# The sums of xT's blocks in the widening stages: from GpSimd to VectorE

## The chip, the core and the metric

The kernel runs on one core of a Trainium2 chip. The metric is the time of one execution on the device, in microseconds (us). In the profile the engines are PE (TensorE's matmuls; PEld is its weight loads), DVE (VectorE), ACT (ScalarE), POOL (GpSimd) and SP (SyncE, which here issues loads from HBM).

## The reference

Two transformer-like blocks are computed on x of 512 tokens by 1024 channels, in float32. What matters here are the three places where a wide pair of projections (1024 to 2 x 2816) feeds a gate:

```python
def swiglu(x, w_gate, w_up, w_down):
    return (jax.nn.silu(x @ w_gate) * (x @ w_up)) @ w_down
...
def _conv_ffn(x, w_in, conv_w, conv_b, w_out):
    s = x.shape[1]
    u = x @ w_in
    up = jnp.pad(u, ((0, 0), (CONV_WIDTH_2 - 1, 0), (0, 0)))
    u = sum(conv_w[j] * up[:, j:j + s] for j in range(CONV_WIDTH_2)) + conv_b
    g, val = u[..., :D_FF_2], u[..., D_FF_2:]
    return (jax.nn.silu(g) * val) @ w_out
```

swiglu is in the first block; _conv_ffn comes twice, once after each attention of the second block.

## The kernel before

Every float32 matmul is three passes on high and low parts (hi x hi, hi x lo, lo x hi): `split` (L182) makes the high part with an ACT copy (L183) and the low part with a subtraction on DVE (L185). Weights come as tiles `raw` (SP loads), are split into `wh` and `wl`, 128x1024 each, and go to PE; a small pool of such pieces is released as PE finishes with them. The normed input, transposed, is in xT: `xh` and `xl`, each in two tiles of four rows of 128 channels (order lists the tiles as xh_5119 and xh_5120 in stage two).

A widening stage is `wide` (L776). There are three: in `block1_ffn` (about 190 to 440 us, "stage one"), and in `conv_ffn` (from about 797 us, "stage two", and from about 1411 us, "stage three"; these two run the same code). Each has 22 chunks of 128 gate and 128 value channels:

- The first four chunks (`f_phase`, the lead) are plain products into PSUM tiles `fa`. In the first two of them PE also turns the last tokens into xT (tiles `pt`).
- The other 18 are `fast_chunk`: a Strassen-like scheme with seven smaller products per chunk instead of eight. In order they use the operands g[2], g[1], g[5], g[6], g[7], g[4], g[3]. Product 1 fills half of PSUM tile `c` (c2), and ACT copies it out to `m` (m2, L519). Product 2 fills tile `p` (p1). Product 3 goes to the other half of c2, and waits for the copy m2.

The operands g are made by `sums` (L465). It first adds high and low parts of xT's four blocks (L474: 4 additions of 128x1024), then makes five sums or differences of these, z1 to z5 (L483: 5 more), kept in unused rows of `hT`. Each z is then split (L183 and L185) into an operand: z1 to `g1h`/`g1l`, z2 to `g6h`/`g6l`, z3 to `g7h`/`g7l`, z4 back into the second tile of xT (g[4]) and z5 into the first (g[3]).

For the weights of the fast chunks, sums are needed too: an accumulating DMA on POOL's queue (L274) and then two additions of 128x512 on POOL (L277 and L278, recorded as L176, `raw`<-`raw`); ACT's copy to `wh` waits for these. In stages two and three POOL also multiplies gate and value (L1011, recorded as L176, `hT`<-`hT`,`tv`), and each PSUM tile is emptied by an ACT pass (L1002) and two DVE passes ("taps", L1003 and L1004). In stage one there is one DVE multiplication (L967) per chunk instead.

The order on each engine is fixed at build time by a scheduler with priorities; PE's order is written out by hand. An engine takes its instructions strictly in that order. `issue_after` and `behind` bind only this order.

Of the kernel before, what the change touches and what calls it, by code (L numbers as in the profile page):

```python
# [99 lines left out]
class Net:  # L100
# [675 lines left out]
    def wide(self, hT, evac):  # L776

        with ExitStack() as fs:
            pool, self.fz = (fs.enter_context(self.tc.tile_pool(name=n, bufs=1)) for n in ("sums", "fz"))
            self.f_phase(LEAD, evac)  # L780

            rows = lambda r: hT[:, r:r + 2, :].rearrange("p a (b c) -> p (a b) c", c=256)
            tmp = [rows(NF - KD + 2 * i) for i in range(4)]
            zs = [lambda i=i: rows(LEAD + 2 * i) for i in range(5)]
            new = lambda n: tuple(pool.tile([P, 4, 256], F32R, name=f"g{n}{e}") for e in "hl")
            b = {}
            with self.behind(3), self.tc.issue_after(self.powed.ins):
                for _ in self.sums(b, new, tmp, zs):
                    pass
            with self.tc.manual_schedule(engines={mybir.EngineType.PE}):  # L790
                for c in range(LEAD, NF):
                    if c == NF - 1:
                        self.operands = 0
                        self.ahead = [self.pair(hT, 0)]
                    ps = {}
                    for _ in self.fast_chunk(b, ps.__setitem__, True):
                        pass
                    evac(c, ps[0], ps[1])
# [774 lines left out]
```

## Time and profile before

| | |
|---|---|
| median of 3 runs | 1767.71 us (1765.19 to 1772.61) |
| the profiled execution: its time | 1769.7 us |
| its span in the trace | 1767.9 us |
| TensorE clock granted, mean of the span | 0.98 |
| PE busy | 1671.8 us, 95% of the span |
| DVE busy | 1438.4 us, 81% |
| ACT busy | 1011.4 us, 57% |
| POOL busy | 757.6 us, 43% |

The span is a little shorter than the time, since the time also holds what lies around the recorded instructions. A busy share is an average over stages with different limits.

### The profile page before, as it was taken

The numbers are of one execution on the slowest core, as the hardware profiler recorded it, in microseconds if no ns is written. First come the engines' busy times: TensorE is split into PE (matmuls) and PEld (weight loads), VectorE is DVE, ScalarE is ACT, GpSimd is POOL, SyncE is SP. The second block draws the span as 40 slices with busy tenths as digits, with TensorE's granted clock in tenths as the row PEclk, the third lists the DMA queues.
The fourth block names the chain that finished last, engine by engine and source line by source line (L and its number), as shares of the span: only waits on it lengthen the run. The fifth ranks groups of instructions, "written<-read, shape, count | busy, mean of one in ns | idle before, by whom it ended". The sixth has DMA issues, their size and how long they took to land. (4 is left out here: it accounts for less than half of the span.)

```text
span 1767.9 us, 28040 instructions
## 1 busy us (share of the span) xinstructions
PE 1671.8 (95%) x10432; PEld 1486.2 (84%) x10432; DVE 1438.4 (81%) x2159; ACT 1011.4 (57%) x1733; POOL 757.6 (43%) x528
## 2 busy tenths in 40 slices
PE   6977999999999999999999998999998999999996
PEld 6856999999788889879999987787776799999875
DVE  5985677678877789967899899855888679998999
ACT  6662445455563677745666564644667455656553
POOL 2485643330023365218555527344232185566522
PEclk9988999999999999989999999999999999999998
DMA  6469566668978665744566689797543335666553
GB/s 233 170 187 246 154 161 179 192 180 282 351 218 220 166 158 149 203 109 136 154 181 178 179 283 333 218 238 193 124 114 89 97 98 156 182 194 185 191 184 107
DMA packets 106072, 326.05 MB, mean 184 GB/s; under 512 B 9888, under 2 KB 10016, under 8 KB 93904
## 3 DMA queue, kind: packets, MB, share of 16 engines
q1 hardware_dynamic: 73088, 215.53, 35.6%
q0 software_dynamic: 25648, 73.54, 22.3%
q10 hardware_dynamic: 7200, 35.20, 5.5%
q8 instruction: 82, 1.34, 0.3%
q14 instruction: 54, 0.44, 0.1%
HBM read 274.91 MB, written 73.43 MB: 197 GB/s over the span
## 5 line engine op out<-in xcount | busy, mean ns | idle before, releaser
L183 ACT ACTIVATE wh<-raw 128x1024 fp32r<-128x1024 f32 x457 | 450.8, 998 | 405.4 <-PE c L437 100.3
L185 DVE TENSOR_TENSOR wl<-raw,wh 128x1024 fp32r<-128x1024 f32 (+1 forms) x415 | 528.4, 1287 | 132.2 <-ACT wh L183 125.8
L436 PE MATMUL c<-xh,wh 128*128 128x256 f32 x992 | 283.5, 286 | 8.8 <-ACT m L519 8.8
L176 POOL TENSOR_TENSOR raw<-raw 128x512 f32<-128x512 f32 x124 | 180.6, 1456 | 247.0 <-DMA raw<-raw 207.3
L437 PE MATMUL c<-xl,wh 128*128 128x256 f32 x992 | 282.5, 285 | 0.0
L438 PE MATMUL c<-xh,wl 128*128 128x256 f32 x992 | 281.9, 284 | 0.0
L436 PEld LDWEIGHTS c<-xh,wh 128*128 128x128 f32 x992 | 190.7, 192 | 10.7 <-ACT m L519 10.5
L437 PEld LDWEIGHTS c<-xl,wh 128*128 128x128 f32 x992 | 190.7, 192 | 0.2
L438 PEld LDWEIGHTS c<-xh,wl 128*128 128x128 f32 x992 | 190.7, 192 | 0.0
L438 PE MATMUL dn<-wh,hl 128*128 128x512 f32 x462 | 181.6, 394 | 7.7 <-DVE hl L185 7.6
L437 PE MATMUL dn<-wl,hh 128*128 128x512 f32 x462 | 181.8, 395 | 2.5 <-DVE wl L185 2.4
L436 PE MATMUL dn<-wh,hh 128*128 128x512 f32 x462 | 179.2, 394 | 0.1
L150 POOL COPY paced<-wh 128x1 f32<-128x1 f32 x48 | 35.6, 741 | 232.1 <-ACT wh L183 232.0
L436 PE MATMUL fa<-xh,wh 128*128 128x256 f32 (+1 forms) x400 | 133.0, 333 | 1.6 <-ACT wh L183 1.6
L437 PE MATMUL fa<-xl,wh 128*128 128x256 f32 (+1 forms) x400 | 132.6, 332 | 1.1 <-DVE xl L185 1.1
L438 PE MATMUL fa<-xh,wl 128*128 128x256 f32 (+1 forms) x400 | 132.5, 331 | 0.8 <-DVE wl L185 0.8
L176 POOL TENSOR_TENSOR wl<-raw,wh 128x1024 fp32r<-128x1024 f32 (+1 forms) x42 | 97.2, 2319 | 83.3 <-ACT wh L183 80.4
L176 POOL TENSOR_TENSOR hT<-hT,tv 128x512 f32<-128x512 f32 x44 | 102.8, 2336 | 37.3 <-DVE tv L1004 37.3
L176 POOL TENSOR_TENSOR rs_r<-rs_t,mhalf 128x1 f32<-128x1 f32 (+1 forms) x40 | 32.0, 800 | 195.1 <-DVE rs_t L326 193.6
L438 PEld LDWEIGHTS dn<-wh,hl 128*128 128x128 f32 x462 | 87.5, 189 | 27.7 <-DVE hl L185 9.7
L437 PEld LDWEIGHTS dn<-wl,hh 128*128 128x128 f32 x462 | 87.8, 190 | 23.7 <-DVE wl L185 5.8
L436 PEld LDWEIGHTS dn<-wh,hh 128*128 128x128 f32 x462 | 87.7, 190 | 18.8 <-ACT wh L183 0.5
(305 smaller groups left out, 4573.7 us busy)
## 6 DMA issues: line engine op xcount, KB each, us to landing
raw<-in_w_conv_dram SPq DMA_DIRECT2D x36, 1024.0 KB, 4.9
mixed<-in_narrow_dram ACTq DMA_DIRECT2D x48, 704.0 KB, 6.5
raw<-raw POOLq DMA_DIRECT2D x62, 512.0 KB, 5.1
raw<-mixed SPq DMA_DIRECT2D x51, 512.0 KB, 5.9
raw<-in_narrow_dram SPq DMA_DIRECT2D x48, 512.0 KB, 5.8
raw<-in_w_ffn_dram SPq DMA_DIRECT2D x18, 1024.0 KB, 4.9
mixed<-in_narrow_dram POOLq DMA_DIRECT2D x24, 704.0 KB, 10.1
mixed<-mixed POOLq DMA_DIRECT2D x24, 704.0 KB, 9.5
```

The costliest lines, as they stand in the source:

```text
L150: paced = self.nc.gpsimd.tensor_copy(m, self.ready[-1][0][:, 0:1].bitcast(F32))
L176: self.pooled = self.nc.gpsimd.tensor_tensor(*args, **kw)
L183: self.copied = self.nc.scalar.activation(hi, src, AF.Copy)
L185: return self.copied, sub(lo, src, hi.bitcast(F32), op=ALU.subtract)
L436: mm(ps, lh, rh, start=first, stop=False)
L437: mm(ps, lh, rl, start=False, stop=False)
L438: mm(ps, ll, rh, start=False, stop=last)
```

## The change

`sums` is given VectorE's tensor_tensor for its additions, where it used GpSimd's.

```diff
@@ def wide
             with self.behind(3), self.tc.issue_after(self.powed.ins):
-                for _ in self.sums(b, new, tmp, zs):
+                for _ in self.sums(b, new, tmp, zs, self.nc.vector.tensor_tensor):
                     pass
```

In `sums` (unchanged) the argument decides who adds:

```python
        gp = engine or self.pool
        for x, (k, q) in zip(tmp, ((A, t), (A, u), (B, t), (B, u))):
            h, l = here(k, q)
            gp(x, h.bitcast(F32), l.bitcast(F32), op=ALU.add)
```

So nine additions of 128x1024 in each of the three stages leave POOL and enter DVE's order. PE's and SP's orders are the same as before; ACT's and DVE's change around the first fast chunk, and POOL's loses the nine rows.

DVE in stage two, a piece of the difference (lines with + are of the change). The place is from the emptying of the lead's second chunk on.

```order
 L1003 SCALAR_TENSOR_TENSOR tv<-fa,vec,tv 128x511
+L474 TENSOR_TENSOR hT<-xh_5119,xl_5121 128x1024
+L1004 SCALAR_TENSOR_TENSOR tv<-fa,vec,tv 128x510
+L474 TENSOR_TENSOR hT<-xh_5119,xl_5121 128x1024
+L474 TENSOR_TENSOR hT<-xh_5120,xl_5122 128x1024
+L185 TENSOR_TENSOR wl<-raw,wh 128x1024
+L1003 SCALAR_TENSOR_TENSOR hT<-fa,vec,hT 128x511
+L474 TENSOR_TENSOR hT<-xh_5120,xl_5122 128x1024
+L1004 SCALAR_TENSOR_TENSOR hT<-fa,vec,hT 128x510
+L483 TENSOR_TENSOR hT<-hT 128x1024
+L185 TENSOR_TENSOR wl<-raw,wh 128x1024
```

The additions now stand between the taps and the weight splits of the lead's chunks, and the other four L483 rows follow in the same manner, all ahead of g1l.

ACT in stage two before, the last rows up to m2 (the row m_8765, which product 3 waits for):

```order
L183 ACTIVATE xh_5119<-hT 128x4x256
L1010 ACTIVATE hT<-hT 128x512
L183 ACTIVATE wh<-raw 128x512
L1002 ACTIVATE tv<-fa,vec 128x512
L183 ACTIVATE xh_5120<-hT 128x4x256
L519 ACTIVATE m_8765<-c_8762 128x256
```

Four instructions stood between the copy of z5 (xh_5119) and m2. The same place in the change:

```order
L183 ACTIVATE g7h<-hT 128x1024
L183 ACTIVATE xh_5119<-hT 128x4x256
L183 ACTIVATE wh<-raw 128x512
L1002 ACTIVATE tv<-fa,vec 128x512
L1010 ACTIVATE hT<-hT 128x512
L183 ACTIVATE xh_5120<-hT 128x4x256
L519 ACTIVATE m_8765<-c_8762 128x256
```

The rows are the same; g7h has moved up to just ahead of xh_5119, and the gate function (L1010) back behind the tap.

## Rows read from the trace of the kernel before

**Rows 1.** The page, part 1: busy time, share of the span, instructions.
```profile
PE 1671.8 (95%) x10432; PEld 1486.2 (84%) x10432; DVE 1438.4 (81%) x2159; ACT 1011.4 (57%) x1733; POOL 757.6 (43%) x528
```

**Rows 2.** PE's waits in stage one, 176 to 340 us: total, times, longest.
```profile
PE pt L337 <- DVE y L357: 0.2, 1, 0.2
```

**Rows 3.** PE's waits in stage two, 780 to 960 us.
```profile
PE c L436 <- ACT m L519: 2.6, 1, 2.6
...
PE pt L337 <- DVE X L391: 0.2, 1, 0.2
```

**Rows 4.** PE's waits in stage three, 1380 to 1560 us.
```profile
PE c L436 <- ACT m L519: 2.9, 1, 2.9
...
PE pt L337 <- DVE X L391: 0.4, 1, 0.4
```

**Rows 5.** PE's timeline around the wait in stage two: start, length, instruction.
```profile
845.84 0.28 PE L437 MATMUL p<-g1l,wh 128*128 128x256 f32 x1
...
849.91 0.39 PE L436 MATMUL c<-xh,wh 128*128 128x256 f32 x1 [2.59 <-ACT m L519]
```

**Rows 6.** Two windows behind the waits: length, busy us (instructions) per engine, PEclk.
```profile
850.90:854.32 3.42, 3.42 (x18) 3.42 (x18) 3.30 (x5) 1.06 (x1) 2.50 (x2) 0.50 0.71 156
1465.31:1468.72 3.41, 3.41 (x18) 3.41 (x18) 2.99 (x4) 1.06 (x1) 2.01 (x2) 0.50 0.87 178
```

**Rows 7.** ACT's timeline in stage two.
```profile
840.40 1.06 ACT L183 ACTIVATE wh<-raw 128x1024 fp32r<-128x1024 f32 x1 [0.26 <-POOL raw L176]
...
843.63 1.05 ACT L183 ACTIVATE xh<-hT 128x1024 fp32r<-128x1024 f32 x1
846.83 0.63 ACT L1010 ACTIVATE hT<-hT 128x512 f32<-128x512 f32 x1 [2.14 <-DVE hT L1004]
...
849.49 0.37 ACT L519 ACTIVATE m<-c 128x256 f32<-128x256 f32 x1
```

**Rows 8.** DVE's timeline in stage two.
```profile
815.08 2.91 DVE L185 TENSOR_TENSOR wl<-raw,wh 128x1024 fp32r<-128x1024 f32 x1 [5.26 <-ACT wh L183]
817.92 0.74 DVE L1003 SCALAR_TENSOR_TENSOR hT<-fa,vec,hT 128x511 f32<-128x511 f32 x1
...
819.36 1.99 DVE L185 TENSOR_TENSOR wl<-raw,wh 128x1024 fp32r<-128x1024 f32 x1
...
828.64 1.65 DVE L185 TENSOR_TENSOR g1l<-hT,g1h 128x1024 fp32r<-128x1024 f32 x1
...
836.68 1.29 DVE L185 TENSOR_TENSOR wl<-raw,wh 128x1024 fp32r<-128x1024 f32 x1 [3.46 <-ACT wh L183]
...
841.49 1.22 DVE L185 TENSOR_TENSOR wl<-raw,wh 128x1024 fp32r<-128x1024 f32 x1 [2.08 <-ACT wh L183]
```

**Rows 9.** POOL's timeline in stage two.
```profile
814.51 12.46 POOL L176 TENSOR_TENSOR hT<-hT 128x1024 f32<-128x1024 f32 x4
826.93 2.28 POOL L176 TENSOR_TENSOR hT<-hT,tv 128x512 f32<-128x512 f32 x1
829.16 1.24 POOL L274 DMA_DIRECT2D raw<-raw  x1
835.59 1.29 POOL L176 TENSOR_TENSOR raw<-raw 128x512 f32<-128x512 f32 x1 [5.20 <-DMA raw<-raw]
```

**Rows 10.** POOL's groups by shape, whole span: the sums of the three stages.
```profile
L176 POOL TENSOR_TENSOR hT<-hT 128x1024 f32<-128x1024 f32 x15 | 47.2, 3176 | 0.2
...
L176 POOL TENSOR_TENSOR hT<-xh,xl 128x1024 f32<-128x1024 f32 x12 | 29.4, 2468 | 2.7 <-PE pt L337 2.7
```

**Rows 11.** The additions of `sums` on DVE in the first attention: ns min/median/max.
```profile
L474 DVE TENSOR_TENSOR sum<-xh,xl x4: 1211/1214/1216, 534.8 to 542.3; 128x1024 f32<-128x1024 f32 x4
...
L483 DVE TENSOR_TENSOR sum<-sum x5: 1214/1216/1226, 544.6 to 572.7; 128x1024 f32<-128x1024 f32 x5
```

**Rows 12.** DVE's timeline in stage one: the split of z1.
```profile
220.70 3.42 DVE L185 TENSOR_TENSOR g1l<-hT,g1h 128x1024 fp32r<-128x1024 f32 x1
```

**Rows 13.** PE's timeline in stage one: product 2 of the first fast chunk.
```profile
238.09 0.28 PE L437 MATMUL p<-g1l,wh 128*128 128x256 f32 x1
```

## Prediction

> **What bounds the kernel now.** I read the page first: PE is busy for 95% of the span, DVE for 81% [rows 1]. So the change can only act on time in which PE waits, and the next view is PE's waits, stage by stage. In stage one there is one of 0.2 us [rows 2]. In stages two and three one wait stands out, 2.6 and 2.9 us, for ACT's copy m2 [rows 3, 4]; the rest is 0.2 and 0.4 us for the normed X before a transposition. The wait has a second price. In the window right behind it the granted clock is 0.50, the lower of the two levels, for 3.41 us in each stage [rows 6]; PE does half as much in it, which loses 1.7 us. So the two waits cost 2.6 + 2.9 + 2 x 1.7 = 8.9 us together, 0.5% of the time, and 9.5 with the small waits for X. This is all that there is to gain.
>
> Why is m2 late? Follow it back through four timelines. ACT ran m2 at 849.49, as the last of a row of instructions that began at 846.83, and that first one had waited 2.14 us for a DVE tap [rows 7]. DVE was late because its weight splits had waited for `wh`, 3.46 us at 836.68 and 2.08 at 841.49 [rows 8]. The second `wh`, at 840.40, had waited for POOL's addition of raw weights [rows 7]; the first of these additions started at 835.59, behind an accumulating DMA that POOL issued at 829.16, and POOL got there only after its sums (the last four ended at 814.51 + 12.46 = 826.97) and one multiplication [rows 9]. So today's wait does begin at the sums on POOL. The question is what takes their place.
>
> **The change, part by part.** *Removed:* 27 additions on POOL, 47.2 + 29.4 = 76.6 us of its time [rows 10]. POOL is not a bound, so this alone is worth nothing; what counts is that the DMA goes out earlier. It still needs its own weights loaded first, into a `raw` buffer that DVE frees with the split at 819.36 [rows 8], so the bounds are no gain and 829.16 - 821.35 = 7.8 us (821.35 is the end of that split). I take 4.5 as an estimate, in the middle: issued near 824.7, landed 6.4 us later as today [rows 9], near 831.
>
> *Added:* nine additions on DVE in each stage. The same operation on the same shape ran there in the first attention, 1.21 us each [rows 11]: 9 x 1.215 = 10.9 us a stage.
>
> *Given back:* two things. Under POOL's sums DVE's weight splits were slow, 2.91 us once and 1.99 three times in stage two, against 1.22 at 841.49 [rows 8]: 1.7 + 3 x 0.77 = 4.0 us come back. And the two waits for `wh`, 3.46 + 2.08 = 5.5 us, can be filled with additions, since `wh` comes earlier; by the new order I expect about 2 us of idle time to stay (before `wh` copies that wait for PE to release pieces or for the landing at 831; the bounds are 0 and the 5.5 of today).
>
> *Moved:* by DVE's new order the splits g1l, g6l and g7l come behind the taps of the last gate tile, where they were ahead of them: 1.65 + 2 x 1.2, some 4 us that no longer delay this tap, but delay g1l itself. In ACT's new order the copy of z5 (xh_5119) is followed by four instructions and then m2, so m2 now hangs on z5, the last addition.
>
> *The unknown:* DVE's additions read two operands from SBUF, as the slow weight splits do, and POOL still has some seven operations of 128x512 in that stretch (multiplications and raw additions). How much each costs DVE is shown by no row of before. Bounds from the nearest rows: nothing at the lower end (the split at 836.68 took 0.07 us more than 1.22 with POOL at work), and 1.29 us each at the upper end, if each addition waits out a whole POOL operation [rows 8, 9]: 0 to 9.0 us. I take 0.3 each, 2 us: between 0.07 and the 0.77 that was seen beside a POOL that ran without a gap, and nearer to the first, since the operations left are short and apart.
>
> *The sum, for stage two.* Let T be the end of the DVE tap that ACT waited for, today about 846.8 [rows 7]. T = 846.8 + 10.9 - 4.0 - 4.1 - 5.5 + 2.0 + 2.0 = 848.1. z5 ends one tap earlier, 0.75 before T. From there ACT needs one split copy, about 1.0 (1.05 in the row at 843.63), and then what it needed from 846.83 to 849.49, 2.66 [rows 7]: m2 starts at T + 2.9 = 851.0, 1.5 us later than today. g1l is ready at T + 1.2 = 849.3, where PE wants it at 845.84 [rows 5]: product 2 now waits 3.5 us as well, and what is left of the wait for m2 stands behind it. The low clock I leave as today. Behind product 3, PE is fed about as it was, since DVE's later splits slide with T. So a stage loses 1.5 us; stage three runs the same code and loses the same.
>
> Stage one: g1l ended at 224.1 while PE wanted it at 238.09 [rows 12, 13]. Even 10.9 us more, with no relief counted, would fit into these 14 us, and DVE has no taps there. I put it at zero.
>
> The small waits for X (0.2 and 0.4) stand under POOL's first sums and shrink: -0.4.
>
> Total: 2 x 1.5 - 0.4 = +2.6 us. The profiled execution took 1769.7, so it would take 1772.3; it lies 2.0 above the median of the runs, 1767.71, on which I put the same difference: **1770.3**.
>
> **Rivals.** *The waits vanish* (faster). If T falls to 844.4 or below, m2 is there when product 2 ends (847.3) and g1l nearly in time. Then both waits, both stretches of low clock and the small waits go: 1767.7 - 9.5 = 1758.2. It needs 3.7 us less than my sum: no idle time left on DVE and hardly a collision. For it speaks that the chain that makes m2 late today begins at POOL; against it, that DVE, which must now do the sums ahead of the same tap, has no room. The Trainium skill's page "GPSIMD Engine Reference" (section "Engine selection") says that additions of two tensors belong on VectorE, GpSimd being about twice as slow. The trace agrees, 1.21 against 2.47 and 3.18 us [rows 10, 11], and by that rule alone this rival would be the outcome. What it leaves out is the queue that the additions join. 0.11.
>
> *The wait splits in two and the clock stays up.* Part falls on product 2 and part on product 3; if neither brings the low clock, 2 x 1.7 comes off: 1766.9. It needs pieces shorter than the 2.6 that was enough for it today, and I expect 3.5 on product 2. 0.20.
>
> *DVE is the new bound* (slower). Place: the same additions; mechanism: collisions with POOL. It decides from 5 us of collisions on, of 9.0 possible: then T is 851.1, a stage loses 4.6, and the total passes +8.8. With 7 us: T = 853.1, 6.6 a stage, 1767.7 + 13.2 - 0.4 = 1780.5. For it speaks the 1.99 and 2.91; against it, that POOL runs with gaps once its sums are gone. 0.14.
>
> **How the numbers follow.** The forecast itself, a small loss of 0 to 8 us, has 0.55. A measurement here can tell about 0.5%, 8.8 us, from no change. The forecast and the split wait lie within it, as do the weak ends of the other two: faster 0.10, same 0.77, slower 0.13. The range goes from 1761 (collisions near nothing, one of the two waits gone) to 1778 (5 us lost a stage), and leaves out the cores of the first and last rivals, 2 in 10.
>
> **What would show it.** In the changed profile: the additions at about 1.2 to 1.6 us on DVE; the accumulating DMA of stage two issued near 825 instead of 829; a PE wait on g1l (DVE, L185) at product 2 and one on m2 behind it, together 3 to 6 us a stage; no new wait in stage one. The forecast is wrong if PE runs through products 2 and 3 without a wait, or if the additions take 2 us and more and PE waits there for 8.

## The result: 1.0% slower, and the profile after

The changed kernel takes 1786.49 us (median of 6 runs, 1780.92 to 1789.14); the kernel before, run beside it, takes 1768.3 (6 runs). The ratio is 1.0098, 95% interval 1.0083 to 1.0113: some 18 us slower. The forecast of 1770.3 and its range, which ended at 1778, are missed. The profiled execution took 1784.89 us, its span is 1782.8.

The page's part 1 after the change answers to [rows 1]:

```profile
PE 1671.0 (94%) x10432; PEld 1485.2 (83%) x10432; DVE 1442.3 (81%) x2186; ACT 1010.9 (57%) x1733; POOL 684.0 (38%) x501
```

POOL is busy 73.6 us less (757.6 before), since its 27 additions are gone. DVE now has them, and yet its total is only 3.9 us higher: its weight splits no longer run beside POOL's sums. By these totals the exchange is a bargain. PE's busy time is the same. The loss must be in what PE waits for, so its waits come next, those of stage one first, then of stages two and three (they answer to [rows 2 to 4]; total, times, longest):

```profile
PE p L437 <- DVE g1l L185: 2.2, 1, 2.2
PE c L438 <- DVE wl L185: 1.0, 1, 1.0
PE c L436 <- DVE y L527: 0.5, 1, 0.5
...
PE p L437 <- DVE g1l L185: 6.9, 1, 6.9
PE c L437 <- DVE xl L185: 1.6, 2, 1.1
...
PE p L437 <- DVE g1l L185: 6.6, 1, 6.6
PE c L437 <- DVE xl L185: 1.7, 2, 1.2
```

The wait for m2 is gone. In its place product 2 waits for g1l, as forecast, but for 6.9 and 6.6 us instead of 3.5, and in stage one too, where nothing was expected. DVE's timeline in stage two shows what g1l stood behind (the answer to [rows 8]):

```profile
815.33 1.22 DVE L185 TENSOR_TENSOR wl<-raw,wh 128x1024 fp32r<-128x1024 f32 x1 [5.26 <-ACT wh L183]
...
821.78 1.67 DVE L185 TENSOR_TENSOR wl<-raw,wh 128x1024 fp32r<-128x1024 f32 x1 [0.89 <-ACT wh L183]
...
826.60 1.22 DVE L474 TENSOR_TENSOR hT<-xh,xl 128x1024 f32<-128x1024 f32 x1
...
828.39 2.35 DVE L474 TENSOR_TENSOR hT<-xh,xl 128x1024 f32<-128x1024 f32 x2
834.73 1.29 DVE L185 TENSOR_TENSOR wl<-raw,wh 128x1024 fp32r<-128x1024 f32 x1 [3.98 <-ACT wh L183]
...
836.60 1.65 DVE L474 TENSOR_TENSOR hT<-xh,xl 128x1024 f32<-128x1024 f32 x1
...
838.84 1.65 DVE L483 TENSOR_TENSOR hT<-hT 128x1024 f32<-128x1024 f32 x1
...
844.13 2.35 DVE L483 TENSOR_TENSOR hT<-hT 128x1024 f32<-128x1024 f32 x2
846.40 2.29 DVE L185 TENSOR_TENSOR wl<-raw,wh 128x1024 fp32r<-128x1024 f32 x1
848.61 0.74 DVE L1003 SCALAR_TENSOR_TENSOR hT<-fa,vec,hT 128x511 f32<-128x511 f32 x1
849.27 1.62 DVE L483 TENSOR_TENSOR hT<-hT 128x1024 f32<-128x1024 f32 x1
850.82 0.73 DVE L1004 SCALAR_TENSOR_TENSOR hT<-fa,vec,hT 128x510 f32<-128x510 f32 x1
851.48 1.63 DVE L185 TENSOR_TENSOR g1l<-hT,g1h 128x1024 fp32r<-128x1024 f32 x1
```

Two things are to be seen. An addition on an undisturbed DVE takes about 1.2 us, as forecast. But after the first three, DVE stands idle for 3.98 us in front of a weight split, with six more additions queued behind it. And several rows are longer than 1.21 (a pair: 2.35): 0.46 + 0.08 + 0.44 + 0.44 + 1.08 + 0.41 + 0.42 = 3.3 us from 821.78 to the end of g1l. The taps, whose first operand is in PSUM, never are.

POOL's timeline says what the split waited for (the answer to [rows 9]), and below it are ACT's copies `wh` and m2 (to [rows 7]):

```profile
825.05 1.24 POOL L274 DMA_DIRECT2D raw<-raw  x1 [2.68 <-issue]
833.65 1.29 POOL L176 TENSOR_TENSOR raw<-raw 128x512 f32<-128x512 f32 x1 [7.36 <-DMA raw<-raw]
834.90 2.27 POOL L176 TENSOR_TENSOR hT<-hT,tv 128x512 f32<-128x512 f32 x1
837.14 2.27 POOL L176 TENSOR_TENSOR raw<-raw 128x512 f32<-128x512 f32 x1
```

```profile
833.64 1.06 ACT L183 ACTIVATE wh<-raw 128x1024 fp32r<-128x1024 f32 x1 [8.02 <-PE fa L437]
...
854.60 0.36 ACT L519 ACTIVATE m<-c 128x256 f32<-128x256 f32 x1
```

The accumulating DMA goes out at 825.05, 4.1 us earlier than before, as forecast (near 825). But it lands only at 833.65, 8.6 us later instead of 6.4: of the 4.1 us gained, 1.9 are left. The copy `wh` starts within a hundredth of it. The row names PE as its releaser, but the run without a first sum and without products, below, shows that PE had freed the piece long before.

Last, the clock in the windows from the wait on (the answer to [rows 6]):

```profile
846.20:848.90 2.70, 0.04 (x1) 0.00 (x0) 2.70 (x3) 1.01 (x2) 2.62 (x2) 1.00 0.00 0
848.90:853.10 4.20, 0.00 (x0) 0.00 (x0) 4.20 (x5) 2.11 (x3) 3.12 (x2) 0.50 0.73 250
853.10:859.14 6.04, 5.98 (x28) 5.98 (x29) 5.03 (x8) 2.75 (x5) 2.80 (x2) 0.50 0.67 133
```

PE stands from 846.2 to 853.1. The granted clock falls to 0.50, its lower level of 1.2 GHz, during the wait, and stays there for 6.04 us of work after it, where it was 3.41 before. So the second price of the wait grew from 1.7 to 3.0 us.

### The profile page after: what moved, and what is told of

It is laid out like the page before. It is cut to its first block, busy times and chain, and to the rows that moved or that the text cites. A ratio compares the mean times of both kernels' runs of the same rounds, so it can differ in the third digit from the quotient of the medians.

```text
span 1782.8 us, 28043 instructions
## 1 busy us (share of the span) xinstructions
PE 1671.0 (94%) x10432; PEld 1485.2 (83%) x10432; DVE 1442.3 (81%) x2186; ACT 1010.9 (57%) x1733; POOL 684.0 (38%) x501
## 5 line engine op out<-in xcount | busy, mean ns | idle before, releaser
L185 DVE TENSOR_TENSOR wl<-raw,wh 128x1024 fp32r<-128x1024 f32 (+1 forms) x415 | 494.1, 1204 | 135.6 <-ACT wh L183 132.2
L274 POOL DMA_DIRECT2D raw<-raw x62 | 74.1, 1195 | 121.5 <-DMA raw<-in_w_ffn_dram 33.0
```

Of the source, the lines that this page charges most:

```text
L185: return self.copied, sub(lo, src, hi.bitcast(F32), op=ALU.subtract)
L274: self.nc.gpsimd.dma_start(out=raw[:, 0:4:2, :], in_=raw[:, 1:4:2, :], accum_op=ALU.add)
```

## Experiments

Two theories. A (order): the additions on DVE stand in a strict order behind a weight split, which waits for the late DMA. B (collisions): DVE's additions and splits and POOL's operations hold each other up, and that is the main cost.

### One stage at a time

```diff
-    def wide(self, hT, evac):
+    def wide(self, hT, evac, engine=None):
...
-                for _ in self.sums(b, new, tmp, zs, self.nc.vector.tensor_tensor):
+                for _ in self.sums(b, new, tmp, zs, engine):
...
-            self.wide(hT, evac)
+            self.wide(hT, evac, nc.vector.tensor_tensor)
```

The last line stands in `block1_ffn` in the first of the two kernels, in `conv_ffn` in the second.

> VectorE makes the sums in stage one alone; GpSimd makes them again in stages two and three. The changed kernel's profile puts 4.6 us of its 18 us loss in stage one: PE waits 2.2 us for g1l, 1.0 for a weight split and 0.5 for y there, where it had waited 0.2. Theory A (order: the additions on VectorE stand behind a weight split that waits for the accumulating DMA) and theory B (collisions of VectorE with GpSimd) both say that stage one pays by itself: 1768 + 4.6 = about 1773 us. The prediction's own step (14 us of slack, so stage one costs nothing) says 1768. The loss of stages two and three is expected to be gone in both.

> VectorE makes the sums in stages two and three; GpSimd makes them again in stage one. If the stages add up, this costs 7.5 + 6.8 = 14.3 us: about 1782.5 us, and with the run of stage one alone the two losses sum to the 18 us of the whole change. If something carries over from stage one into the later ones (or the other way), they don't sum: under 1780 or over 1786.

Stage one alone: 1774.2 us, ratio 1.0027 (1.0015 to 1.0039), 4.8 us of 1768.75. Stages two and three alone: 1785.15 us, ratio 1.0083 (1.0067 to 1.0098), 14.7 us. The two sum to 19.5, against 17.3 for the whole change (0.98% of the same 1768.75); the intervals are some 2 us wide on either side, so the stages add up. In the first kernel PE's waits in stage one are those of the change (2.2, 1.0, 0.5) and those of stages two and three are the old ones (2.7 for m2). So the prediction's zero for stage one is wrong, whatever happens in the later stages.

### The first weight sum as an addition on POOL

```diff
-        self.nc.gpsimd.dma_start(out=raw[:, 0:4:2, :], in_=raw[:, 1:4:2, :], accum_op=ALU.add)
+        gp(raw[:, 0:4:2, :], raw[:, 0:4:2, :], raw[:, 1:4:2, :], op=ALU.add) if first else self.nc.gpsimd.dma_start(out=raw[:, 0:4:2, :], in_=raw[:, 1:4:2, :], accum_op=ALU.add)
```

`first` is true for the first weight block of each widening stage. DVE's, ACT's and PE's orders are those of the change.

> The changed kernel, but the first weight sum of each widening stage, an accumulating DMA, is one addition of 128x1024 on GpSimd; VectorE's, ScalarE's and PE's orders are the same as in the change. Theory A (the late DMA holds the copy wh, this holds a weight split on VectorE, and this holds the additions behind it, 4.0 us in stage two and 5.6 in stage one): the split no longer waits, product 2 waits some 4 us less in stages two and three, the stretch at the low clock becomes shorter, and the wait of stage one goes. 1786.5 - 3.7 - 2 x (4 to 7.4) = 1768 to 1775 us. Theory B (collisions are the main cost): one more operation of GpSimd with two operands in the same stretch, so no gain or a loss: 1786 to 1791 us.

1783.74 us, ratio to the kernel before 1.0085 (1.007 to 1.01): hardly better than the change. Theory A expected at most 1775 and falls as it stood; theory B expected 1786 or more and is missed too. The profile says why. DVE's timeline in stage two, and POOL's below it:

```profile
824.11 3.27 DVE L185 TENSOR_TENSOR wl<-raw,wh 128x1024 fp32r<-128x1024 f32 x1
...
827.96 1.66 DVE L474 TENSOR_TENSOR hT<-xh,xl 128x1024 f32<-128x1024 f32 x1
...
830.20 3.88 DVE L474 TENSOR_TENSOR hT<-xh,xl 128x1024 f32<-128x1024 f32 x2
834.01 1.21 DVE L185 TENSOR_TENSOR wl<-raw,wh 128x1024 fp32r<-128x1024 f32 x1
...
850.80 1.21 DVE L185 TENSOR_TENSOR g1l<-hT,g1h 128x1024 fp32r<-128x1024 f32 x1
```

```profile
823.91 6.87 POOL L176 TENSOR_TENSOR raw<-raw 128x1024 f32<-128x1024 f32 x3 [2.24 <-issue]
830.73 2.28 POOL L176 TENSOR_TENSOR hT<-hT,tv 128x512 f32<-128x512 f32 x1
```

The stall in front of the split at 834.01 is gone, as A said. But POOL's three additions run just where DVE's do, and DVE's rows are now 7.1 us over length, instead of 3.3 (0.45 in a split at 821.10, 2.06 + 0.45 + 1.53 in the rows above, then 1.10, 0.44 and 1.08 up to g1l). One loss took the place of the other, and product 2 still waits 6.5 us for g1l. In stage one the same edit did help: the wait for g1l is gone and 0.5 us each for a weight split and for y are left. There too collisions took the place of the stall (the four L474 rows run for 9.02 us instead of 4.63), but by less: 6.0 us of rows over length, against 5.62 of stall and 3.3 over length in the change.

### Leaving the losses out, one by one

To see both losses apart, POOL's work was left out. Without the lead's products of gate and value:

```diff
-                self.pool(g, g, v, op=ALU.mult)
+                c < LEAD or self.pool(g, g, v, op=ALU.mult)
```

> The changed kernel without GpSimd's products of gate and value for the lead's four chunks in stages two and three (so part of the hidden layer is not gated). The DMA and GpSimd's weight sums stay. By the changed trace some 0.9 us a stage of the 2.9 us of collisions lie beside these products, and the wait of VectorE behind the DMA, 4.0 us, stays. If VectorE is simply full (every us of stall ahead of g1l falls on the tensor engine), the wait for g1l goes from 6.9 to about 6.0 us: 1783 to 1786 us. If collisions were the main cost, it would be halved: under 1780.

Without the first block's weight sums:

```diff
-        self.nc.gpsimd.dma_start(out=raw[:, 0:4:2, :], in_=raw[:, 1:4:2, :], accum_op=ALU.add)
+        first or self.nc.gpsimd.dma_start(out=raw[:, 0:4:2, :], in_=raw[:, 1:4:2, :], accum_op=ALU.add)
...
-            gp(two[:, 1, :], raw[:, 2, :], raw[:, 1, :], op=ALU.add)
-            gp(two[:, 2, :], two[:, 1, :], two[:, 0, :], op=ALU.add)
-            return [two[:, 1:3, :].rearrange("p s c -> p (s c)")], None
+            for j, x, y in [] if first else [(1, raw[:, 2, :], raw[:, 1, :]), (2, two[:, 1, :], two[:, 0, :])]:
+                gp(two[:, j, :], x, y, op=ALU.add)
+            return [flat[:, 1024:] if first else two[:, 1:3, :].rearrange("p s c -> p (s c)")], None
```

> The changed kernel without any sum for the first weight block of each widening stage: neither its accumulating DMA nor its two additions on GpSimd (so the first fast chunk multiplies unsummed weights). Last time the DMA's stall was removed, and three additions on GpSimd came in its place with 7.2 us of collisions against 2.9. Here both go, and what is left are GpSimd's products, about 2.6 us a stage. If stall and collisions are two parts of one bound, a full VectorE, the wait for g1l goes from 6.5 to about 2 us, with a short stretch at the low clock or none: 1764 to 1774 us. If neither is the cause: 1782 us or more.

And with both edits:

> Both left out, the first block's weight sums and the lead's products: VectorE has its additions, splits and taps and nearly nothing to collide with. Its work from the split at 821.1 on to the end of g1l is 23.9 us without a stall, so g1l would be there at about 845, when product 2 wants it (845.8): no wait for g1l, 1759 to 1768 us. If a wait of several us stays, the additions cost more than stalls and collisions explain.

They took 1785.28 us (ratio 1.0099, 1.0074 to 1.0123), 1775.64 (1.0045, 1.0032 to 1.0058) and 1766.31 (0.9991, 0.9976 to 1.0007). The third equals the kernel before. The second lies a little above its 1764 to 1774: its wait was 2.9 us and not about 2. In stage two, with the over-length rows added up as above:

| kernel | DVE idle before the split that the DMA held | rows over length, to g1l's end | sum | PE's wait for g1l |
|---|---|---|---|---|
| the change | 4.0 | 3.3 | 7.3 | 6.9 |
| no products | 5.3 | 2.1 | 7.4 | 6.9 |
| first sum on POOL | 0 | 7.1 | 7.1 | 6.5 |
| no first sum | 0 | 3.6 | 3.6 | 2.9 |
| neither | 0 | 1.2 | 1.2 | 0.6 |

The last column is read from PE's waits in stage two; below are the rows of the last four kernels, in this order:

```profile
PE p L437 <- DVE g1l L185: 6.9, 1, 6.9
PE p L437 <- DVE g1l L185: 6.5, 1, 6.5
PE p L437 <- DVE g1l L185: 2.9, 1, 2.9
PE p L437 <- DVE g1l L185: 0.6, 1, 0.6
```

The wait is the sum less 0.4 to 0.7 us in all five. Stage three repeats this with another mixture: in the change the stall is 2.98 us there (the DMA took 7.9) and 4.0 us are over length, 7.0 together, for a wait of 6.6; with neither, 1.1 us are over length and the wait is 0.4. So DVE, with the sums in this place, has about half a us of slack before product 2 wants g1l, and whatever holds it, a stall or a collision, reaches PE in full. This is the result of the study. Theories A and B are two parts of one bound, and neither is the cause alone.

Two rows need a word. The run without products met its number (1783 to 1786) by luck, for another reason than expected: the collisions shrank by 1.2 us, but its DMA landed 9.7 us after its issue and the stall grew by 1.3. And the run with neither has this in DVE's timeline:

```profile
829.27 1.22 DVE L185 TENSOR_TENSOR wl<-raw,wh 128x1024 fp32r<-128x1024 f32 x1
...
844.65 1.21 DVE L185 TENSOR_TENSOR g1l<-hT,g1h 128x1024 fp32r<-128x1024 f32 x1
```

The split that had waited 3.98 us follows the additions without a gap. Its copy `wh` starts at 827.23, when PE frees a piece; so in the changed kernel, which is 0.95 us later there (its split at 815.33 against 814.38), PE had freed it by about 828.2, and the 5.4 us to 833.64 were the DMA's.

### Another order in the same place

```diff
-            with self.behind(3), self.tc.issue_after(self.powed.ins):
+            with self.behind(3), self.tc.issue_after(self.powed.ins), self.tc.high_priority(offset=250):
```

> The changed kernel with the additions and the splits g1l, g6l and g7l at high priority, still held behind the third group of later work: the additions stand in a row, one weight split between the fourth and the fifth, then the three splits, and the taps that stood between them come after. The sum of VectorE's work from there to the copy m2 is the same. Full VectorE: the wait for g1l goes, but the taps are later, so the lead's PSUM tiles or m2 are late instead: 1778 to 1788 us. If only the place of g1l behind the last tap cost the time: 1768 us or less.

1792.93 us, ratio 1.0145 (1.0117 to 1.0172): above the full-DVE theory's 1778 to 1788, but by its mechanism. The wait for g1l is gone in stages two and three (in stage one product 2 waits 3.6 us for a weight split instead), but the taps now stand behind the sums, and the lead's PSUM tiles come free late (stage two):

```profile
PE fa L436 <- DVE tv L1004: 12.1, 1, 12.1
```

It is longer than the wait it replaced, since all eight taps stand behind nine additions and three splits. A stretch of 13.65 us at the low clock began within it. So this other arrangement of the same work in the same place only moved the wait; no third one was tried.

### Another place

```diff
-            with self.behind(3), self.tc.issue_after(self.powed.ins):
+            with self.tc.issue_after(self.powed.ins):
```

> The changed kernel, but the scheduler isn't told to hold the additions behind the third group of later work, so they stand on VectorE right after (partly between) the splits that make xT, where it was idle for 5.3 us in stage two and 8.3 in stage one; the split g6l comes earlier too. Theory A (a place in the order decides): additions and splits no longer wait behind the weight split that the DMA holds, and g1l and m2 are ready in time: 1762 to 1772 us, so most of the loss is gone. Theory B (collisions): only the collisions of the additions, 2.9 us a stage by the sum over stage two, can go: 1786.5 - 3 x 2.9 = 1778 us or more. A loss beyond 1787 would say that the splits of xT, now partly behind additions, make PE wait at the start of the lead.

1761.95 us (9 runs), ratio to the kernel before 0.9958 (0.9945 to 0.9971): 7.4 us faster than before and, by the medians, some 24 faster than the change. PE's waits in stage two, and DVE's timeline there:

```profile
PE fa L437 <- DVE xl L185: 0.6, 1, 0.6
PE c L436 <- ACT m L519: 0.2, 1, 0.2
```

```profile
802.21 1.21 DVE L474 TENSOR_TENSOR hT<-xh,xl 128x1024 f32<-128x1024 f32 x1
...
812.96 1.23 DVE L474 TENSOR_TENSOR hT<-xh,xl 128x1024 f32<-128x1024 f32 x1
...
814.70 1.21 DVE L483 TENSOR_TENSOR hT<-hT 128x1024 f32<-128x1024 f32 x1
...
833.71 1.28 DVE L185 TENSOR_TENSOR wl<-raw,wh 128x1024 fp32r<-128x1024 f32 x1 [1.85 <-ACT wh L183]
...
836.23 2.25 DVE L185 TENSOR_TENSOR g1l<-hT,g1h 128x1024 fp32r<-128x1024 f32 x1
```

Six additions now run from 802 to 817. There DVE had idled for want of weights (5.26 us before 815.33 in the changed kernel), and POOL, with nothing to do between 807.4 and 825.9, leaves them at 1.17 to 1.23 us. Only three stand later. The split still waits for the DMA, 1.85 us, but g1l ends at 838.5, long before it is wanted. The stretch at the low clock is gone with the wait. DVE's busy time is the change's, 1442.3 us to the tenth. (This edit moves some of PE's instructions too: the last eight transpositions stand behind 65 of the lead's products in this trace, and behind 48 in the changed kernel's.)

Two more runs bound this. The same release with the sums on POOL (the edit above, in the kernel before):

> The kernel before (sums on GpSimd), with the same release as the run of the early sums: nothing holds the sums behind the third group of later work. By the order GpSimd's own row stays as it was, and on VectorE the splits g6l, g1l and g7l move up to right behind xT's last split, ahead of the lead's first weight splits. Does the early place pay by itself, without VectorE's additions? Theory (place and engine belong together): the sums need some 29 us on GpSimd, so these splits wait until about 830 in stage two, the lead's weight splits wait behind them, and the tensor engine stands for 12 to 20 us a stage and more at the low clock: 1768 + 3 x (12 to 25) = 1804 to 1843 us. If the place alone gave the gain: 1765 us or less.

1797.64 us, ratio 1.0164 (1.0137 to 1.0191): the early place costs 28 us without the fast engine. The mechanism is the expected one, but smaller than expected: the split g6l waits 8.20 us for POOL's sums, with the lead's weight splits behind it, and PE waits 8.1 us for the lead's tiles in stage two. And the early sums on DVE together with the first weight sum on POOL:

> The early sums on VectorE, and the first weight sum of each stage as one addition on GpSimd in place of the accumulating DMA. VectorE's order is that of the early sums. In that run the tensor engine's waits in the three stages are down to 0.2 and 0.6 us, so there is nothing left to win: 1760 to 1764 us, the same as the early sums alone (1762) if the stall behind the DMA (1.9 us on VectorE there) has become slack. If the added collisions reach g1l, 1765 us or more.

1762.2 us, ratio 0.996 (0.9944 to 0.9977): the same as the early sums alone. With DVE's work moved away, the stall behind the DMA is slack.

## Why the prediction was wrong, point by point

- **What bounds the kernel, and what would follow m2.** Right in the main. PE lost its time at product 2, on g1l, and the wait for m2 disappeared behind it, wholly, where the sum had left 2.6 + 1.5 - 3.5 = 0.6 us of it. The DMA went out near 825, and an addition costs about 1.2 us (a pair 2.35). One reading was incomplete: before the change PE also waits 0.6 us for xl of the lead in each of stages two and three, which "all that there is to gain" leaves out. These waits are there after the change too.
- **The step that failed: "about 2 us of idle time to stay".** It was 0.22 + 0.89 + 3.98 = 5.1 us in stage two. The mis-sized part of this term is the landing: the estimate put it at 831, with 6.4 us from issue to landing as in [rows 9]; it took 8.6 and came at 833.65. DVE had three additions behind it at 830.74 and then needed `wh`, which takes 1.06: by these rows a landing at 831.1 would have left a stall of some 1.4 us instead of 3.98, and an idle time of about 2.5. The split that hangs on the landing stands on DVE in the middle of the sums, six of them behind it, so the whole delay went on to g1l. Why the DMA took longer stays open.
- **Collisions: 2.0.** Too small, but not the main error in stage two. Up to the last tap they were 2.9 (3.3 less the 0.42 of g1l): within the bounds of 0 to 9.0, 0.9 over the value taken. T was forecast at 848.1 and came at 851.55, on a timeline that ran 0.25 later (815.33 against 815.08 at the first split). Of the 3.2 us between, the idle term makes 3.1 and collisions 0.9; the nine additions at some 1.14 us from start to start instead of 1.215 take 0.7 back.
- **"The low clock I leave as today", and "Behind product 3, PE is fed about as it was".** Both wrong. The wait grew from 2.6 to 6.9, the work done at the low level from 3.41 to 6.04 us, and behind product 3 PE now waits 1.6 us for xl, the late splits of z4 and z5. Together this makes a stage 4.3 + 1.6 + 1.3 = 7.2 us dearer, where the forecast had 1.5; the run with these two stages alone gives 14.7 / 2 = 7.4.
- **"Stage one: I put it at zero."** Wrong by 4.8. The 14 us of slack [rows 12, 13] held 10.9 us of additions, but not also a stall of 5.62 us behind a DMA that landed 9.4 us after its issue (219.43 to 228.82), and 3.3 us of rows over length (three additions in 4.58 us, one in 2.31 with its split g1l in 2.29). With the DMA replaced, the two came to 6.0 us instead of 8.9, and the wait of 2.2 us for g1l went. The stall stands in DVE's timeline of the change:

```profile
219.68 4.63 DVE L474 TENSOR_TENSOR hT<-xh,xl 128x1024 f32<-128x1024 f32 x4
229.93 1.26 DVE L185 TENSOR_TENSOR wl<-raw,wh 128x1024 fp32r<-128x1024 f32 x1 [5.62 <-ACT wh L183]
```

- **The rivals.** "DVE is the new bound" (1780.5, chance 0.14) was nearest, in good part by luck. T did pass its point of decision (851.1; T was 851.55), but not by its mechanism: it wanted 5 us of collisions, and 2.9 came up to T, the rest was idle time. Its sum has a slip: by the prediction's own terms T = 851.1 and 853.1 cost 4.5 and 6.5 us a stage, not 4.6 and 6.6, which gives 1780.3. What "The waits vanish" describes came in another kernel, at 1762, once the additions stood where DVE was idle. The rule of the Trainium skill's page "GPSIMD Engine Reference" (section "Engine selection"), additions on VectorE, is borne out by the engine's own time here; it paid in one place and lost 1% in another.
- **What would show it.** The length of the additions and the DMA's issue came as named; the wait of 6.9 us at product 2 (3 to 6 were named), the missing wait on m2 and the new waits in stage one did not. Neither of its signs of being wrong came: PE did wait, and the additions took 1.2 to 1.65 us, not 2 and more. A loss that is made up of several terms, each somewhat larger, had no sign of its own.

## What to carry to other kernels

Work that moves to an in-order engine must be placed, not only priced: find that engine's idle stretch and the instructions of its order that wait for others, and put the work ahead of them. If the engine is full up to a deadline, every stall and every collision there adds to the wait one for one, and removing one of them can bring the other; measure them apart before choosing which to remove. A transfer that goes out earlier may meet other transfers; do not take over its old duration unasked (6.4 us became 8.6 here).

## What was not expected of the hardware

- The accumulating DMA of 512 KB took 6.4 us from issue to landing in stage two before the change and 8.6 after, 5.7 and 9.4 in stage one, 9.7 in stage two without products, and 5.5 there with the early sums. In the three slowest of these cases SP issued its next load of 1 MB 0.4 to 1.0 us behind the DMA (826.05 behind 825.05 in stage two); in the others that load went out 1.1 or 2.2 us ahead of it, or 2.3 behind. Two cases in between took 7.9 us: stage three of the change, with the load 1.3 behind, and stage one of the early sums, with the load 0.3 ahead. The two loads around the DMA of stage two took 5.8 us in the mean instead of 4.8. That the two share something is the reading that this suggests; it was not tested by itself and stays open.
- Operations of DVE with two operands in SBUF ran up to 3.42 us instead of 1.21 beside POOL (the split of z1 in [rows 12]), and POOL's of 128x512 around the sums up to 4.41 us (one product in the run without a first sum) instead of 1.30. Taps, with one operand in PSUM, stayed at 0.73 to 0.75 throughout. The Trainium skill's page "SBUF — State Buffer" (section "Who interferes with whom") says this: a VectorE instruction with two inputs in SBUF contends with a GpSimd instruction that reads SBUF, and one with at most one such input does not, outside the modes that use both of VectorE's ports. The traces agree for splits, additions and taps. But one operation with a single tensor in SBUF was slow beside POOL as well: the TENSOR_SCALAR of L391 took 2.89 us under POOL's sums (at 801.35 in the kernel before) and 0.81 in the change; whether it ran in such a mode no run shows.
- The stretch at the low clock was longer behind longer waits, though not strictly. At product 2 or 3: none with waits of 0.2 and 0.6 us, nor with 2.2 in stage one of the change; 3.41 us with 2.6 to 2.9; 6.83 or 10.24 us with 6.2 to 7.7. At the lead's tiles: 6.83 us with 8.1 in the run of the early sums on POOL, 13.65 with 12.1 and 12.9 in the run of the sums in a row.
